# Weights of three projections moved by 4 to 28 bytes (a few by 128 or 256) against the operand that streams past them, and three raw buffers in place of four

## The chip, the cores and the metric

One core of one Trainium2 chip runs the whole program. The metric is the device time of one execution in microseconds, median of several runs.

## The reference

The reference is a decoder trunk of four layers over 256 tokens of width 1024. Each layer has a token mixer (Mamba-2 in layers 0 and 3, a gated linear recurrence in layer 1, a gated delta rule in layer 2), a cross-attention into 256 memory tokens, and a gated MLP. Cut to what matters here:

```python
for i in range(DEPTH):
    hn = rmsnorm(x, ln_mix[i])
    mix = (mamba2_mixer, hgrn2_mixer, gated_deltanet_mixer)[i % 3](hn, ...)   # begins with hn @ in_w, ends with @ out_w
    x = x + mix
    x = x + memory_cross_attention(rmsnorm(x, ln_xattn[i]), rmsnorm(mem, ln_mem[i]), ...)
    x = x + conv_glu_ffn(rmsnorm(x, ln_ffn[i]), f_up[i], f_conv_w[i], f_conv_b[i], f_down[i])

def conv_glu_ffn(h, up_w, conv_w, conv_b, down_w):
    gate, up = jnp.split(h @ up_w, 2, axis=-1)
    gate = causal_dwconv(gate, conv_w) + conv_b
    return (jax.nn.silu(gate) * up) @ down_w
```

All of it is float32. The weights of `in_w` (of the Mamba mixer), `up_w` and `down_w` are the ones the change touches; the kernel calls them `m_in`, `f_up` and `f_down`.

## The kernel before, in words

Every large product is done as three products of a shorter float format (float32r). A float32 operand is split into a high part H, which ScalarE writes as a cast, and a low part L, the rest, which VectorE writes as a difference; then `mm3` (lines 166 to 170) adds H·H, H·L and L·H into one PSUM bank. So one tile of weights of 128x1024 costs 24 matmuls: eight slices of 128 columns are loaded one after the other as the stationary operand, and 256 tokens stream past each of them three times.

`prep` (lines 152 to 164) brings such a tile in. It takes a buffer `raw` out of a ring of `WB[0]` = 4, one `wH` out of 3 and one `wL` out of 3, loads 512 KB over SyncE's queue (line 159), casts on ScalarE (line 160) and subtracts on VectorE (line 161). The framework adds the waits: a load waits until the difference that read its raw buffer is done, a cast waits until the matmuls that read its `wH` are done. `prep` runs at a higher priority than what stands around it, so the scheduler puts its load, cast and difference early on each engine's queue; each engine then works strictly in the order of its queue, SyncE's too.

The users of `prep` that matter here are these. `proj` (line 229) multiplies the layer's normalized input `hH`, `hL` with two tiles at a time; the Mamba mixer calls it for `m_in` (line 619, eight groups g of six tiles in each of layers 0 and 3, into the bank `mps`) and the MLP for `f_up` (line 475, 44 tiles per layer, bank `ffps`). `out_proj` (line 254) multiplies a mixer's or the MLP's result, split into `aH` and `aL`, with `f_down` (and other weights) in groups of four tiles, into the four banks `acc`; in the MLP it has six groups, the last of half size. The other products with weights (`xa_kv`, `xa_q`, `xa_o`, `h_in`, `g_in`, `g_out`, `m_out`, `h_out`) use the same `prep`.

Where the tiles lie in a partition of SBUF is settled when the program is built. Here the buffers `raw`, `wH` and `wL` begin at multiples of 512 bytes; `hH`, `hL`, `aH`, `aL` and the memory's `mH`, `mL` begin 192 bytes past such a multiple (the tile `apad` of 48 floats puts `aH` there). A slice of weights is 512 bytes long and a row of tokens 1024. So in nearly every product of `mm3` the address of the streamed operand less that of the loaded one is 192 modulo 512 bytes, and this number is what "distance" means in this document. It is 320 where the weights stream and the tokens are loaded (half of `xa_kv`, and one part of `h_in`), and 0 in the scores of the attention (bank `sc`).

The delta-rule mixer of layer 2 (lines 829 to 1126) needs a small triangular inverse per head: VectorE makes `MT`, SyncE's queue writes it to a DRAM scratch `gd` (line 927) and reads blocks of it back as `blk` (line 928), GpSimd works on them and writes them to DRAM, and SyncE's queue brings `U` back (line 958). These loads stand in the same queue as the raw loads. Around them a class `Weave` lets the heads' small matmuls slip between the projections' matmuls by a clock of its own.

Of the kernel before, what the change touches and what calls it, by code (L numbers as in the profile page):

```python
# [9 lines left out]
F32R = mybir.dt.float32r  # L10
# [6 lines left out]
P = 128  # L17
D = 1024
T = 256
# [3 lines left out]
NFF = 22  # L23
# [63 lines left out]
def tile_trunk(ctx: ExitStack, tc: tile.TileContext, io: dict, out: bass.AP, layers=range(DEPTH), parts="mxf", final=True):  # L87
    nc = tc.nc
    ACT, DVE, POOL, PE = nc.scalar, nc.vector, nc.gpsimd, nc.tensor
    weave = Weave()  # L90
    WB = [4,3,3]
    HL = [607, 282, 1973, 470, 14335, 1000]
    NL = [9214]
    LAT = [21000, 5620, 1450, 1042, 1588, 1117, 1724, 2353, 942, 2058, 8335, 1093, 4452, 2125, 1556]
# [6 lines left out]
    wp = ctx.enter_context(tc.tile_pool(name="wp", bufs=3))  # L101
# [12 lines left out]
    def bank(name):  # L114
        return ps_acc.tile([P, 512], F32, tag="acc", name=name)
# [8 lines left out]
    def f32(ap):  # L124
        return ap.bitcast(F32)
# [23 lines left out]

    between = []  # L150

    def prep(src, n=1024, step=1024):
        with tc.high_priority(offset=PRIO):
            raw = wp.tile([P, 1024], F32, tag="raw", name="raw", bufs=WB[0])
            H = wp.tile([P, 1024], F32R, tag="wH", name="wH", bufs=WB[1])
            L = wp.tile([P, 1024], F32R, tag="wL", name="wL", bufs=WB[2])
            for o in range(0, n, step):
                c = slice(o, min(n, o + step))
                nc.sync.dma_start(out=raw[:, c], in_=src[:, c])
                ACT.copy(H[:, c], raw[:, c])  # L160
                DVE.tensor_tensor(out=L[:, c], in0=raw[:, c], in1=f32(H[:, c]), op=ALU.subtract)  # L161
                if len(between) > 1:
                    between[-1](between.pop(0))
        return H, L

# [5 lines left out]

    def split(src, H, L):
        return (ACT.copy(H, src), DVE.tensor_tensor(out=L, in0=src, in1=f32(H), op=ALU.subtract))  # L173

# [5 lines left out]

    def split_gain(src, g, H, L):

# [43 lines left out]
        yield 440, 0  # L226


    def proj(srcs, ps):

        for i, s in enumerate(srcs):
            H, L = prep(s)
            for kt in range(KT):
                c = slice(kt * P, (kt + 1) * P)
                mm3(ps[:, i * T:(i + 1) * T], H[:, c], L[:, c], hH[:, kt, :], hL[:, kt, :],
                    i == 0 and kt == 0, kt == KT - 1)
                if kt % 2:
                    weave.tick(654)
# [12 lines left out]
                    if k % 2:  # L251
                        weave.tick(654)

    def out_proj(wsrc, nk, a, gens=None, gname=None, layer=0, last=False):


        accs = [bank(f"acc{b}") for b in range(4)]
        ng = (nk + 3) // 4
        st = Stats(DVE if last else POOL)
        for g in range(ng):  # L260
            n = min(4, nk - 4 * g)
            if gens is not None:
                weave.finish(gens[g])
            aH, aL = [], []
            for k in range(0, n, 2):
                H = ap_.tile([P, 2, T], F32R, tag="aH", name="aH")
                L = ap_.tile([P, 2, T], F32R, tag="aL", name="aL")
                split(a[:, 4 * g + k:4 * g + k + 2, :], H, L)
                aH += [H[:, 0, :], H[:, 1, :]]
                aL += [L[:, 0, :], L[:, 1, :]]  # L270
            for b in range(4):
                H, L = prep(wsrc[g, b], n * T)
                for cb in range(2):
                    for k in range(n):
                        kt = 4 * g + k
                        c = slice(k * T + cb * P, k * T + (cb + 1) * P)
                        mm3(accs[b][:, cb * T:(cb + 1) * T], H[:, c], L[:, c], aH[k], aL[k],
                            kt == 0 and cb == 0, kt == nk - 1)
                        if k % 2:
                            weave.tick(654)  # L280
                if g == ng - 1:
                    xs = flat(xT[:, 2 * b:2 * b + 2, :])
                    DVE.tensor_tensor(out=xs, in0=xs, in1=accs[b], op=ALU.add)
                    if gname is not None:
                        for kt in (2 * b, 2 * b + 1):
                            split_gain(xT[:, kt, :], pcol(gname, layer * 8 + kt), hH[:, kt, :], hL[:, kt, :])
                    st.add(xs)
                    if last:
                        for kt in (2 * b, 2 * b + 1):
                            fg = pcol("final", kt)  # L290
                            if b < 3:
                                POOL.tensor_scalar(out=KTt[:, kt, :], in0=xT[:, kt, :], scalar1=fg, scalar2=None, op0=ALU.mult)
                            else:
                                ACT.activation(out=KTt[:, kt, :], in_=xT[:, kt, :], func=AF.Copy, scale=fg)
        return st
# [161 lines left out]
    def ffn(layer, st, hook=None, last=False):  # L457
        with ExitStack() as ex:
            wk = ex.enter_context(phase(f"ff{layer}", 2))
            aT = wk.tile([P, NFF, T], F32, name="aT", bufs=1)  # L460
            rs = np_.tile([P, T], F32, tag="nrs", name="nrs", bufs=1)
            def gate(t, ps):
                gu = wk.tile([P, 2, T], F32, tag="gu", name="gu")
                DVE.tensor_tensor(out=gu, in0=ps.rearrange("p (a b) -> p a b", a=2),
                                  in1=rs.unsqueeze(1).to_broadcast([P, 2, T]), op=ALU.mult)
                c = wk.tile([P, T], F32, tag="c", name="c")
                conv(c, gu[:, 0, :], lambda j: pcol("f_cw", (layer * NFF + t) * 3 + j), 3, pcol("f_cb", layer * NFF + t))
                silu = ACT.activation(out=c, in_=c, func=AF.Silu)
                DVE.tensor_tensor(out=aT[:, t, :], in0=c, in1=gu[:, 1, :], op=ALU.mult)
                return silu  # L470

            todo = []
            for t in range(NFF):
                ps = bank("ffps")
                proj([io["f_up"][layer, 2 * t + i] for i in range(2)], ps)
                todo.append((t, ps))
                if t == 0:
                    continue
                if t == 1:
                    st.rs(rs)  # L480
                for u in todo:
                    silu = gate(*u)
                todo = []
                if t == 6 and hook is not None:
                    hook(silu)
            exp_ln_tables(silu)
            return out_proj(io["f_down"][layer], NFF, aT, last=last)

    def softplus(u, n, tmp):

# [18 lines left out]
    def mamba(layer, ia, gname):  # L509
        with ExitStack() as ex:  # L510
# [5 lines left out]
            H, L = prep(io["m_dt"][ia], 256)  # L516
# [94 lines left out]
            gens = []  # L611
            for g in range(8):
# [3 lines left out]
                Es = [wk.tile([P, 384], F32, tag=f"E{k}", name="E") for k in range(4)]  # L616
                for u in range(3):
                    ps = bank("mps")
                    proj([io["m_in"][ia, 6 * g + 2 * u + i] for i in range(2)], ps)
                    with tc.high_priority(offset=EVAC):  # L620
                        if u == 2:
                            exp_ln_tables(ACT.activation(out=bx, in_=cc, func=AF.Silu),
# [537 lines left out]
    for i, l in enumerate(layers):  # L1160
# [7 lines left out]
        else:  # L1168
            for kt in range(KT):
                g = "ln_xattn" if "x" in parts else "ln_ffn"  # L1170
# [13 lines left out]
    for b in range(4):  # L1184
        o = Vt.rearrange("p a (b t) -> p (a b) t", t=T)[:, 2 * b:2 * b + 2, :]
# [125 lines left out]
```

## Time and profile before

| | us |
|---|---|
| median of 3 runs | 2073.72 (2066.06 to 2088.24) |
| the profiled execution | 2072.47 |
| its span, first to last instruction | 2070.7 |
| TensorE busy | 2025.5 |
| VectorE busy | 1590.6 |
| ScalarE busy | 1282.5 |
| GpSimd busy | 344.5 |

The mean granted clock of TensorE was 0.997. TensorE's matmuls are recorded from the moment they begin to stream until their result is written, so one lasts longer (about 280 ns) than the step to the next; PE is the row of the matmuls, PEld that of the weight loads. A row of the timeline gives the start, the duration, the engine, the line and the names "written <- read".

### The profile page before, as it was taken

To read this page: it belongs to the slowest core of one execution; us is meant where nothing else is said; L and a number is where in the kernel's file an instruction comes from. 1 tells how busy PE (TensorE), PEld (TensorE's weight loads), DVE (VectorE), ACT (ScalarE), POOL (GpSimd) and SP (SyncE) were. 2 spreads that over 40 slices of the span, in tenths; PEclk is the share of its full clock that TensorE was granted. 3 is DMA by queue.
4 is the path that set the end of the run, shared out by engine and by line. 5 is a ranking of instruction groups with operands and counts; after the bars stand their busy time and mean duration, and the time that the engine had idled before them with its cause. 6 is when DMAs were issued, how large, how long until landed. Compare 5 with 4: busy or idle time off the path is not lost.

```text
span 2070.7 us, 42162 instructions
## 1 busy us (share of the span) xinstructions
PE 2025.5 (98%) x17084; PEld 1971.5 (95%) x17084; DVE 1590.6 (77%) x2423; ACT 1282.5 (62%) x1874; POOL 344.5 (17%) x468
## 2 busy tenths in 40 slices
PE   8999999999999999999999999999999999999997
PEld 8999999999999899999988889999999999999997
DVE  6899787875688777866786775778757999778765
ACT  6677666654565566555676875666545777666553
POOL 2032211000132110001064451110000223201001
PEclk9999999999999999999999999999999999999999
DMA  7554555655654446666543333456656444545663
GB/s 239 163 155 152 162 154 162 206 188 170 206 157 140 149 137 195 203 195 192 186 130 126 114 113 115 139 163 211 195 179 196 151 154 150 174 133 183 186 189 115
DMA packets 110372, 343.10 MB, mean 166 GB/s; under 512 B 15456, under 2 KB 25312, under 8 KB 110176
## 3 DMA queue, kind: packets, MB, share of 16 engines
q1 hardware_dynamic: 106176, 333.42, 52.0%
q10 hardware_dynamic: 3744, 6.71, 1.0%
q8 instruction: 134, 2.20, 0.4%
q0 software_dynamic: 256, 0.26, 0.1%
q14 instruction: 62, 0.51, 0.1%
HBM read 336.42 MB, written 3.93 MB: 164 GB/s over the span
## 4 chain that ended last, share of the span: by engine, by line
PE 79%; DVE 6%; issue 5%; ACT 4%; DMA 3%; POOL 2%; ACTq 0%; SPq 0%; DVEq 0%; POOLq 0%
PE acc L168 7%; PE ffps L170 7%; PE acc L169 7%; PE ffps L169 7%; PE ffps L168 7%; PE acc L170 7%; PE mps L168 4%; PE mps L169 4%; PE mps L170 4%; DVE wL L161 2%; PE kvps L170 2%; PE kvps L168 2%; PE kvps L169 2%; PE qps L170 2%; PE qps L168 2%
## 5 line engine op out<-in xcount | busy, mean ns | idle before, releaser
L161 DVE TENSOR_TENSOR wL<-raw,wH 128x1024 fp32r<-128x1024 f32 (+2 forms) x639 | 776.1, 1216 | 318.9 <-ACT wH L160 316.6
L160 ACT CAST wH<-raw 128x1024 fp32r<-128x1024 f32 (+2 forms) x639 | 658.4, 1031 | 510.6 <-PE ffps L169 156.4
L168 PE MATMUL acc<-aH,wH 128*128 128x256 f32 x1408 | 396.4, 282 | 0.6 <-ACT aH L173 0.6
L170 PE MATMUL ffps<-hH,wL 128*128 128x256 f32 x1408 | 392.6, 279 | 1.8 <-DVE wL L161 1.7
L168 PE MATMUL ffps<-hH,wH 128*128 128x256 f32 x1408 | 392.0, 279 | 2.5 <-ACT hH L183 2.5
L170 PE MATMUL acc<-aH,wL 128*128 128x256 f32 x1408 | 393.0, 279 | 0.0
L169 PE MATMUL acc<-aL,wH 128*128 128x256 f32 x1408 | 392.4, 279 | 0.1
L169 PE MATMUL ffps<-hL,wH 128*128 128x256 f32 x1408 | 392.1, 279 | 0.2
L168 PEld LDWEIGHTS ffps<-hH,wH 128*128 128x128 f32 x1408 | 265.5, 189 | 3.4 <-ACT hH L183 3.3
L168 PEld LDWEIGHTS acc<-aH,wH 128*128 128x128 f32 x1408 | 265.2, 189 | 3.5 <-issue 1.3
L170 PEld LDWEIGHTS ffps<-hH,wL 128*128 128x128 f32 x1408 | 264.4, 188 | 4.1 <-DVE wL L161 3.7
L169 PEld LDWEIGHTS acc<-aL,wH 128*128 128x128 f32 x1408 | 265.6, 189 | 1.5 <-issue 0.5
L169 PEld LDWEIGHTS ffps<-hL,wH 128*128 128x128 f32 x1408 | 265.1, 188 | 1.1 <-DVE hL L184 0.6
L170 PEld LDWEIGHTS acc<-aH,wL 128*128 128x128 f32 x1408 | 264.6, 188 | 0.4 <-DVE wL L161 0.2
L168 PE MATMUL mps<-hH,wH 128*128 128x256 f32 x768 | 219.8, 286 | 0.0
L170 PE MATMUL mps<-hH,wL 128*128 128x256 f32 x768 | 215.0, 280 | 0.0
L169 PE MATMUL mps<-hL,wH 128*128 128x256 f32 x768 | 214.9, 280 | 0.0
L203 POOL TENSOR_TENSOR ns<-nsq 128x256 f32<-128x256 f32 x13 | 10.5, 811 | 856.5 <-ACT nsq L200 856.5
L168 PEld LDWEIGHTS mps<-hH,wH 128*128 128x128 f32 x768 | 145.1, 189 | 2.7 <-issue 2.4
L170 PEld LDWEIGHTS mps<-hH,wL 128*128 128x128 f32 x768 | 145.4, 189 | 0.1
L169 PEld LDWEIGHTS mps<-hL,wH 128*128 128x128 f32 x768 | 144.5, 188 | 0.3
L170 PE MATMUL gps<-hH,wL 128*128 128x256 f32 x448 | 127.2, 284 | 0.9 <-DVE wL L161 0.9
(397 smaller groups left out, 4489.9 us busy)
## 6 DMA issues: line engine op xcount, KB each, us to landing
raw<-f_up SPq DMA_DIRECT2D x176, 512.0 KB, 3.6
raw<-m_in SPq DMA_DIRECT2D x96, 512.0 KB, 3.5
raw<-f_down SPq DMA_DIRECT2D x80, 512.0 KB, 3.5
raw<-xa_kv SPq DMA_DIRECT2D x60, 512.0 KB, 4.2
raw<-g_in SPq DMA_DIRECT2D x48, 512.0 KB, 3.9
raw<-m_out SPq DMA_DIRECT2D x32, 512.0 KB, 3.5
raw<-xa_q SPq DMA_DIRECT2D x32, 512.0 KB, 3.5
raw<-xa_o SPq DMA_DIRECT2D x32, 512.0 KB, 3.5
```

The source lines that it names most:

```text
L160: ACT.copy(H[:, c], raw[:, c])
L161: DVE.tensor_tensor(out=L[:, c], in0=raw[:, c], in1=f32(H[:, c]), op=ALU.subtract)
L168: PE.matmul(dst, aH, bH, start=start, stop=False, skip_group_check=True)
L169: PE.matmul(dst, aH, bL, start=False, stop=False, skip_group_check=True)
L170: PE.matmul(dst, aL, bH, start=False, stop=stop, skip_group_check=True)
L203: self.eng.tensor_tensor(out=self.sum, in0=sq[:, :T], in1=sq[:, T:], op=ALU.add)
```

## The change

Two things are changed. The ring of raw buffers has three tiles in place of four. And `wH` and `wL` become 512 bytes longer each, with the weights put o elements into them, where o is chosen by a new argument `far`: the distance is then `far` in place of 192. `m_in` gets one distance for each of the eight groups in each of its two layers (144 matmuls each), `f_up` one for each half of its 22 steps in each layer (528 each), and `f_down` one for each half of its groups in each layer (288 for the first, 240 for the second). Together these are 2304 + 4224 + 2112 = 8640 of the 15512 matmuls of the float32r kind. All other products keep 192, 320 or 0 (and the small `m_dt` and `g_ba`, whose slices are 128 and 192 bytes long, the distances that change from slice to slice): what lies behind the weights moves down by 1024 bytes, a multiple of 512.

```diff
-    WB = [4,3,3]
+    WB = [3,3,3]
...
+    FAR = 192
+    UP = [(176, 184), (188, 196), (200, 208), (216, 168)]
+    DOWN = [(196, 200), (208, 188), (184, 176), (448, 320)]
+    MIN = [(164, 168, 172, 176, 180, 184, 188, 448), (196, 200, 204, 208, 212, 216, 220, 64)]
+
+    def prep(src, n=1024, step=1024, far=FAR):
+        o = (FAR - far) % 512 // 4
         with tc.high_priority(offset=PRIO):
             raw = wp.tile([P, 1024], F32, tag="raw", name="raw", bufs=WB[0])
-            H = wp.tile([P, 1024], F32R, tag="wH", name="wH", bufs=WB[1])
-            L = wp.tile([P, 1024], F32R, tag="wL", name="wL", bufs=WB[2])
+            H = wp.tile([P, 1152], F32R, tag="wH", name="wH", bufs=WB[1])[:, o:o + 1024]
+            L = wp.tile([P, 1152], F32R, tag="wL", name="wL", bufs=WB[2])[:, o:o + 1024]
...
-    def proj(srcs, ps):
+    def proj(srcs, ps, far=FAR):
...
-            H, L = prep(s)
+            H, L = prep(s, far=far)
...
-    def out_proj(wsrc, nk, a, gens=None, gname=None, layer=0, last=False):
+    def out_proj(wsrc, nk, a, gens=None, gname=None, layer=0, last=False, fars=(FAR, FAR)):
...
-                H, L = prep(wsrc[g, b], n * T)
+                H, L = prep(wsrc[g, b], n * T, far=fars[2 * g // ng])
...
-                proj([io["f_up"][layer, 2 * t + i] for i in range(2)], ps)
+                proj([io["f_up"][layer, 2 * t + i] for i in range(2)], ps, UP[layer][2 * t // NFF])
...
-            return out_proj(io["f_down"][layer], NFF, aT, last=last)
+            return out_proj(io["f_down"][layer], NFF, aT, last=last, fars=DOWN[layer])
...
-                    proj([io["m_in"][ia, 6 * g + 2 * u + i] for i in range(2)], ps)
+                    proj([io["m_in"][ia, 6 * g + 2 * u + i] for i in range(2)], ps, MIN[ia][g])
```

The order of the instructions stays as it is over most of the program. TensorE's differs in one stretch alone, in the delta-rule mixer. SyncE's queue differs there too. At its beginning, around the load of the first inverse (`U` from the scratch `gd_12485`), SyncE has before:

```order
L159 DMA raw<-g_in 128x1024 x4
L958 DMA U<-gd_12485 128x4x128
L159 DMA raw<-g_in 128x1024
L927 DMA gd_12484<-MT 128x4x128
L928 DMA blk<-gd_12484 32x16x16
L159 DMA raw<-g_in 128x1024 x3
L958 DMA U<-gd_12486 128x4x128
```

and after (lines 8 higher):

```order
L167 DMA raw<-g_in 128x1024 x3
L966 DMA U<-gd_12485 128x4x128
L167 DMA raw<-g_in 128x1024
L935 DMA gd_12484<-MT 128x4x128
L167 DMA raw<-g_in 128x1024
L936 DMA blk<-gd_12484 32x16x16
L167 DMA raw<-g_in 128x1024 x3
L966 DMA U<-gd_12486 128x4x128
```

One raw load that stood ahead of `U` now stands two places behind it. At the mixer's end, where the loads of its output weights `g_out` begin, SyncE has before:

```order
L958 DMA U<-gd_12486 128x4x128
L159 DMA raw<-g_in 128x1024 x2
L159 DMA raw<-g_out 128x1024 x2
L927 DMA gd_12483<-MT 128x4x128
L159 DMA raw<-g_out 128x1024
L928 DMA blk<-gd_12483 32x16x16
```

and after:

```order
L966 DMA U<-gd_12486 128x4x128
L167 DMA raw<-g_in 128x1024 x3
L167 DMA raw<-g_out 128x1024
L935 DMA gd_12483<-MT 128x4x128
L167 DMA raw<-g_out 128x1024
L936 DMA blk<-gd_12483 32x16x16
```

The sequence is the same, shifted by one load.

## Rows read from the trace of the kernel before

**Rows 1.** Page: busy us (share of span) and instructions of each engine.

```profile
PE 2025.5 (98%) x17084; PEld 1971.5 (95%) x17084; DVE 1590.6 (77%) x2423; ACT 1282.5 (62%) x1874; POOL 344.5 (17%) x468
```

**Rows 2.** Groups of instructions on PE, 440 to 520 us.

```profile
L169 PE MATMUL acc<-aL,wH 128*128 128x256 f32 x174 | 48.9, 281 | 0.0
```

**Rows 3.** Groups of instructions on PE, 880 to 950 us.

```profile
L169 PE MATMUL acc<-aL,wH 128*128 128x256 f32 x168 | 46.4, 276 | 0.0
```

**Rows 4.** Timeline of ScalarE, layer 0's MLP, 460 to 472 us.

```profile
464.16 1.05 ACT L160 CAST wH<-raw 128x1024 fp32r<-128x1024 f32 x1 [0.16 <-PE acc L169]
466.98 1.05 ACT L160 CAST wH<-raw 128x1024 fp32r<-128x1024 f32 x1 [1.77 <-PE acc L169]
```

**Rows 5.** Timeline of ScalarE, layer 1's MLP, 905 to 925 us.

```profile
909.35 1.05 ACT L160 CAST wH<-raw 128x1024 fp32r<-128x1024 f32 x1 [1.67 <-PE acc L169]
912.07 1.05 ACT L160 CAST wH<-raw 128x1024 fp32r<-128x1024 f32 x1 [1.67 <-PE acc L169]
```

**Rows 6.** Busy time by stretch: us, PE busy (matmuls), granted clock, DMA share, GB/s.

```profile
346.00:386.00 40.00, 40.00 (x355) 1.00 0.65 205
...
440.00:520.00 80.00, 80.00 (x681) 1.00 0.57 178
...
880.00:950.00 70.00, 70.00 (x620) 1.00 0.62 182
...
1480.00:1540.00 60.00, 60.00 (x531) 1.00 0.59 181
1900.00:1980.00 80.00, 80.00 (x682) 1.00 0.61 188
1985.00:2055.00 70.00, 70.00 (x597) 1.00 0.50 160
```

**Rows 7.** Groups by form on PE, 60 to 76 us (Mamba mixer, layer 0).

```profile
L169 PE MATMUL mps<-hL,wH 128*128 128x256 f32 x45 | 12.4, 276 | 0.0
```

**Rows 8.** Groups by form on PE, 1640 to 1760 us (Mamba mixer, layer 3).

```profile
L169 PE MATMUL mps<-hL,wH 128*128 128x256 f32 x277 | 77.7, 280 | 0.0
```

**Rows 9.** Tile sc, PE: duration ns min/median/max, first and last start.

```profile
L169 PE MATMUL sc<-k1L,qH x16: 283/283/283, 293.0 to 1831.8; 128*128 128x256 f32 x16
```

**Rows 10.** Tile dtps, PE and PEld, loads of 32 columns.

```profile
L169 PEld LDWEIGHTS dtps<-hL,wH x16: 107/108/109, 56.6 to 1596.5; 128*32 128x32 f32 x16
L169 PE MATMUL dtps<-hL,wH x16: 276/276/280, 56.7 to 1596.6; 128*32 128x256 f32 x16
```

**Rows 11.** Tile acc, PEld, loads of 128 columns, 440 to 570 us.

```profile
L168 PEld LDWEIGHTS acc<-aH,wH x176: 187/188/188, 458.3 to 520.1; 128*128 128x128 f32 x176
```

**Rows 12.** Groups by form on VectorE: differences and convolution taps.

```profile
L304 DVE SCALAR_TENSOR_TENSOR cc<-mps,prm,cc 128x255 f32<-128x255 f32 x64 | 30.5, 476 | 0.1
...
L304 DVE SCALAR_TENSOR_TENSOR cc<-mps,prm,cc 128x253 f32<-128x253 f32 x64 | 30.3, 474 | 0.9
```

**Rows 13.** Timeline of VectorE, layer 1's MLP, 905 to 925 us.

```profile
910.43 1.23 DVE L161 TENSOR_TENSOR wL<-raw,wH 128x1024 fp32r<-128x1024 f32 x1 [1.49 <-ACT wH L160]
```

**Rows 14.** Page: DMA issues, count, KB each, median us to landing.

```profile
raw<-f_down SPq DMA_DIRECT2D x80, 512.0 KB, 3.5
```

**Rows 15.** Waits of SyncE's queue: us in total, times, longest us.

```profile
SPq L159 <- DVE wL L161: 1235.3, 470, 7.0
...
SPq L958 <- DMA gd<-ub: 88.6, 8, 16.1
```

**Rows 16.** Timeline of SyncE's queue in the delta-rule mixer.

```profile
1062.99 2.16 SPq L159 DMA_DIRECT2D raw<-g_in  x3
1081.31 0.38 SPq L958 DMA_DIRECT2D U<-gd  x1
```

**Rows 17.** Busy by stretch, delta-rule mixer: us, PE, PEld, DVE, ACT, POOL, clock, DMA, GB/s.

```profile
1070.00:1080.00 10.00, 9.98 (x88) 9.54 (x88) 6.27 (x11) 5.57 (x9) 8.15 (x20) 1.00 0.00 0
1080.00:1090.00 10.00, 8.14 (x65) 7.20 (x64) 4.89 (x10) 4.26 (x7) 3.64 (x6) 1.00 0.57 153
1090.00:1100.00 10.00, 7.64 (x52) 7.43 (x52) 5.50 (x9) 4.49 (x6) 8.26 (x23) 0.83 0.43 171
```

More of the change, by code (lines that the diff above doesn't have):

```diff
@@ L150, in tile_trunk @@
     between = []
-    def prep(src, n=1024, step=1024):
+    FAR = 192
[4 more added lines that the diff above has]
+        o = (FAR - far) % 512 // 4
         with tc.high_priority(offset=PRIO):
             raw = wp.tile([P, 1024], F32, tag="raw", name="raw", bufs=WB[0])
-            H = wp.tile([P, 1024], F32R, tag="wH", name="wH", bufs=WB[1])
-            L = wp.tile([P, 1024], F32R, tag="wL", name="wL", bufs=WB[2])
+            H = wp.tile([P, 1152], F32R, tag="wH", name="wH", bufs=WB[1])[:, o:o + 1024]
+            L = wp.tile([P, 1152], F32R, tag="wL", name="wL", bufs=WB[2])[:, o:o + 1024]
             for o in range(0, n, step):
```

## The prediction

> **What bounds the kernel now.** I read the page's first part first: matmuls cover 98% of the span and weight loads 95%, VectorE 77%, ScalarE 62% [rows 1]. Nobody is waited for long, so the time is the number of matmuls times the step from one to the next, plus small gaps.
>
> Then I looked at that step, by groups of instructions in stretches. The same instruction of the same shape lasts 281 ns in layer 0's MLP and 276 ns in layer 1's, with no idle time ahead of it in either [rows 2, 3] and a granted clock of 1.00 in both [rows 6], the level of 2.4 GHz. ScalarE's casts show what that means for the step: a cast starts when 24 matmuls have freed its buffer, and the casts are 2.82 us apart in the one and 2.72 us in the other [rows 4, 5]. So the step is 117.5 ns or 113.3 ns. I call these the slow and the fast level; they differ by 4.2 ns. The reader is to see that both occur at one and the same distance, 192, that a level lasts for hundreds of matmuls, and that it changes only at a disturbance: counts by stretch are at the fast level until 386 us (355 in 40 us), at the slow one from 440 to 520 (681 in 80), fast through layers 1 and 2 (620 in 70, 531 in 60), slow in layer 3 (682 in 80, 597 in 70) [rows 6]. In the Mamba mixers `m_in` is fast at the beginning (276 ns) and mostly slow later (280 ns, four of the five ns) [rows 7, 8]. So the distance alone does not settle the level here; some phase between weight load and stream does.
>
> Two more rows bear on it. At distance 0, the attention's scores, a matmul lasts 283 ns at the median of the group shown, a third level [rows 9]; by the same proportion (7 ns against 5 for a step of 4.2) its step is 5.9 ns above the fast one. And for `m_dt`, whose loads are of 32 columns (108 ns in place of 188 [rows 10, 11]) and whose distances are 192, 64, 448 and 320 in turn, it lasts 276 ns at the median [rows 10]. Four distances and a far shorter load give no step below the fast level. I take 113.3 ns as the floor of this shape.
>
> **The change part by part.** The sum is made on the profiled execution, 2072.5 us: 2070.7 of span and 1.8 around it. The median of the runs, 2073.7, is 0.1% above.
>
> *The distances.* They touch 8640 matmuls. How many of these are slow now: in layer 0 those from about 400 to 520 us, 120 / 0.1175 = 1020; in layer 3's MLP all 1584; of the 2304 for `m_in` all but the first 133, at four fifths, some 1740. Together 4340, half of the 8640. If every new distance gave the fast level, the gain would be 4340 x 4.2 ns = 18.2 us. If every one gave the slow level, the loss would be the other 4300 x 4.2 ns = 18.1 us. If every one gave the level of distance 0, the loss would be 8640 x 5.9 ns - 18.2 us = 33 us. No row shows a distance between 160 and 220 other than 192, so these are the ends. I take 0, the middle of the first two: 32 pieces of 144 to 528 matmuls at as many distances should fall on both levels, as 192 itself does, and the nearest rows are those of 192, half and half.
>
> *What weights off the old grid cost.* Distances such as 164 or 196 start the weights a few bytes past a 16-byte multiple. For ScalarE and VectorE, which write these tiles, I take nothing: taps of the convolution that write one and three floats off the tile's start take 476 and 474 ns [rows 12], and both engines have slack. For the weight load no row shows such a start. From above: 128 columns take 188 ns and 32 take 108 [rows 10, 11], 0.83 ns for each column, so a load that had to fetch four columns' worth more would take 3.3 ns more. Not counting distances divisible by 16, 5952 matmuls are touched (1728 of `m_in`, 3168 of `f_up`, 1056 of `f_down`): 19.6 us. From below: nothing, or a gain counted above already. I take 0, because a load 80 ns shorter did not shorten the step [rows 10]: at the fast level the load's length isn't what ends last.
>
> The Trainium skill, in "SBUF — State Buffer" under "Specifications (TRN2)", says that SBUF is read in lines of 16 bytes and that each cross to a new line pays a penalty. Weights that start inside a line would cross one line more per load; no row here shows whether that is felt, and by that rule the sum would lean to the upper end of 19.6 us.
>
> *Three raw buffers in a steady stretch.* The load of a tile is issued when the difference of the tile four before is done; SyncE's queue waits for VectorE 470 times, 1235 us in total [rows 15], and that wait is harmless now. With three it is issued one tile earlier in the ring: after the difference that ends at 910.43 + 1.23 = 911.66 us [rows 13], for the cast three steps after 909.35, at 909.35 + 3 x 2.72 = 917.51 [rows 5]. That leaves 5.85 us, of which landing takes 3.5 [rows 14]: 2.3 us to spare, against 5.1 now. So the cover holds, by half its size. Where other loads share the queues (the program's start, the memory's loads in each MLP) it can fail for a tile or two: 0 to 4 us, and I take 1, since three `wH` buffers still stand between a late cast and TensorE.
>
> *Three raw buffers in the delta-rule mixer.* Here SyncE's queue stands still for `U`, 88.6 us in 8 waits, the longest 16.1 [rows 15], and no raw load behind it is issued. The reader can see one such wait: three raw loads are issued by 1065.2, and `U` follows at 1081.3 [rows 16]. TensorE lives on its stock (9.98 of 10 us busy with no DMA at all), then falls to 8.14 and 7.64, and the granted clock to 0.83 [rows 17]. The stock is now one tile smaller, 24 steps, 2.7 us. It costs that for each wait that outlasts the stock. Ends: at most half of the eight, 11 us, since their mean of 11.1 lies well under the longest; and below, a gain of 2.7 us where the shifted order lets a head's chain start a tile earlier. I take one such stall and one drop of the clock like that of the row (10 us x 0.17 = 1.7 us): 4.4 us.
>
> Sum: 2072.5 + 0 + 0 + 1 + 4.4 = 2077.9, rounded 2078 us. The first term's ends alone, all fast and all slow, put it at 2060 and 2096; all ends together at 2052 (2072.5 - 18.2 - 2.7) and 2140 (2072.5 + 33 + 19.6 + 4 + 11).
>
> **The rivals.** *All fast.* Each new distance takes away the slow level. For it: a level is stable for a thousand matmuls, so it is a property of how load and stream meet, and an address shifts that. Against it: distances 192 and 320 have not done it, and `m_in` falls to the slow level again and again. It gives 2077.9 - 18.2 = 2060 us, and 2054 without the raw ring's 5.4; even that is within 1% of before, because of the floor.
>
> *Locked slow.* Load and stream meet badly at most of the new distances, at the slow level or at that of distance 0. For it: 283 ns at distance 0 shows that a distance can hold a level [rows 9]. Against it: 192, 64, 448 and 320 all reach 276 ns. It gives 2077.9 + 18.1 = 2096 us if all are slow, and 2111 if all are like distance 0; it decides the sign from 16.6 us (2094.5 less 2077.9), when the mean step of the 8640 is (18.2 + 16.6) / 8640 = 4.0 ns above the fast level: nearly all slow, or fewer slow with some at the third level.
>
> *Longer loads.* The 3.3 ns of the off-grid start are paid in full: 2077.9 + 19.6 = 2098 us. Against it stands the 32-column load that gained nothing.
>
> *The distance does nothing.* The levels come from the stalls alone, every stretch keeps the level that it has, and only the ring counts: 2078 us, 2073 to 2084.
>
> The Trainium skill, in "TensorE: Matmul & The Clock Gate" under "Step-by-step: what each phase is for", says that TensorE has two independent read ports and that loading the next weights takes nothing from the matmul that runs. By that rule the last rival holds and no distance could matter. The trace speaks against it in part: 283 ns at distance 0 beside 276.
>
> **How the numbers follow.** Mixed levels, my forecast: 0.45, with its own range 2064 to 2094. All fast 0.12. Locked slow 0.20, longer loads 0.10, distance without effect 0.13. About 1% is what a measurement of this kernel can tell from no change, 20.7 us: below 2053 or above 2094.5. Faster by that much needs all fast and a gain in the delta-rule mixer: 0.05. Slower needs locked slow (three quarters of it), longer loads (most of it) or a bad end of the mixed case: 0.27. The same: 0.68. The range reaches from all fast to two thirds of the way into locked slow: 2058 to 2106 us.
>
> **What would show it.** The matmuls' mean duration by group and stretch: 276, 281 or 283 ns for `ffps` by layer and half, for `mps` by group and for `acc`. Right, if both 276 and 281 appear among the new distances and no group of a thousand matmuls lies above 283. Wrong, if a duration below 276 appears with a step below 113.3 ns (then the floor is none), or if off-grid groups lie at 284 and aligned ones (176, 208, 448) at 281 or less (longer loads). For the ring: casts in layer 1's MLP still released by TensorE, not by a DMA, and in the delta-rule mixer PE's busy time in its 290 us lower by 2 to 6 us. The prediction fails as a whole if the time is under 2058 or over 2106.

## The result, and the profile after

| | before | after |
|---|---|---|
| median, us | 2074.89 (2063.97 to 2088.24, 16 runs) | 2092.49 (2089.39 to 2098.16, 16 runs) |
| the profiled execution | 2072.47 | 2090.15 |
| its span | 2070.7 | 2088.3 |

The ratio of after to before is 1.0094, with a 95% interval of 1.0074 to 1.0113: the change makes the kernel 0.9% slower (the two medians alone give 1.0085). The spread is as telling as the median: the changed kernel's runs lie within 9 us, those of before within 24.

The page of after, first part, beside [rows 1]:

```profile
PE 2042.6 (98%) x17084; PEld 1990.5 (95%) x17084; DVE 1590.6 (76%) x2423; ACT 1282.8 (61%) x1875; POOL 342.0 (16%) x468
```

The counts and the shares on TensorE are as before, and PE is busy 17.1 us longer (2042.6 less 2025.5), nearly all of the 17.6 us that the span grew. TensorE's idle time is as long as before in sum (45.7 us of the span against 45.2), though, as shown below, not in the same places. So the same matmuls take longer.

Which of them, the windows of after show, beside [rows 6]. The columns are us, PE busy (matmuls), PEld, DVE, ACT, POOL, granted clock, DMA share, GB/s. From the top: `f_up` at 184, 196, 200, 208, 216 and 168, then `f_down` at 448 and 320:

```profile
405.00:455.00 50.00, 50.00 (x425) 50.00 (x425) 39.06 (x55) 25.73 (x36) 0.00 (x0) 1.00 0.64 198
...
845.00:895.00 50.00, 50.00 (x421) 50.00 (x420) 38.42 (x54) 25.49 (x36) 0.00 (x0) 1.00 0.65 190
1391.00:1441.00 50.00, 50.00 (x425) 49.95 (x424) 40.86 (x61) 31.91 (x48) 0.00 (x0) 1.00 0.62 200
1452.00:1502.00 50.00, 50.00 (x427) 50.00 (x426) 38.72 (x54) 25.86 (x36) 0.00 (x0) 1.00 0.63 191
1903.00:1953.00 50.00, 50.00 (x420) 49.95 (x420) 41.09 (x59) 30.56 (x44) 0.00 (x0) 1.00 0.58 183
1962.00:2012.00 50.00, 50.00 (x444) 50.00 (x443) 40.07 (x57) 26.68 (x37) 0.00 (x0) 1.00 0.63 193
...
2020.00:2048.00 28.00, 28.00 (x249) 28.00 (x248) 15.48 (x16) 15.12 (x17) 0.00 (x0) 1.00 0.65 190
2052.00:2074.00 22.00, 22.00 (x197) 22.00 (x196) 10.58 (x13) 8.59 (x11) 0.28 (x1) 1.00 0.38 121
```

TensorE is busy all through each of them and the clock is granted in full. A window also counts the two or three matmuls that reach over its edges (0.28 us each, 2.4 steps), so 50 / (444 - 2.4) = 113.2 ns a step at 168, 117.8 to 118.3 at 208, 200 and 184 (427, 425), and more at 196 (421, 119.4 ns) and 216 (420). Such a count can be off by one or two at the edges; ScalarE's casts, 24 matmuls apart, don't depend on that. In after, beside [rows 4, 5], with `f_down` at 188 first and `f_up` at 168 below:

```profile
945.49 1.05 ACT L168 CAST wH<-raw 128x1024 fp32r<-128x1024 f32 x1
948.33 1.05 ACT L168 CAST wH<-raw 128x1024 fp32r<-128x1024 f32 x1 [1.79 <-PE acc L177]
...
1962.66 1.05 ACT L168 CAST wH<-raw 128x1024 fp32r<-128x1024 f32 x1 [1.35 <-PE ffps L177]
1965.38 1.05 ACT L168 CAST wH<-raw 128x1024 fp32r<-128x1024 f32 x1 [1.17 <-PE ffps L177]
```

2.84 / 24 = 118.3 ns and 2.72 / 24 = 113.3. The casts are still released by TensorE, in layer 1 and layer 3 alike, and not by a DMA.

`m_in` in after, groups by form at 60 to 76 us and at 1640 to 1760, beside [rows 7, 8]:

```profile
L177 PE MATMUL mps<-hL,wH 128*128 128x256 f32 x45 | 12.7, 281 | 0.0
...
L177 PE MATMUL mps<-hL,wH 128*128 128x256 f32 x273 | 76.6, 281 | 0.0
```

What was 276 ns at the beginning is 281 now, and the 280 of layer 3 are 281.

The rest of the time is in the delta-rule mixer. A window over the whole of it, from its first projection matmul to its last, in after:

```profile
1006.00:1240.00 234.00, 218.19 (x1763) 205.44 (x1762) 181.67 (x360) 175.65 (x262) 95.97 (x221) 0.99 0.42 130
```

and in before:

```profile
1003.00:1233.00 230.00, 218.31 (x1761) 205.17 (x1760) 184.92 (x364) 175.16 (x262) 101.81 (x228) 0.99 0.41 127
```

The work is the same, 218 us, and the idle time goes from 11.7 to 15.8 us. Where it is, the waits of TensorE in after say (waiter, releaser: us in total, times, longest):

```profile
PE l L891 <- ACT gsq L888: 7.6, 1, 7.6
```

And one window of after there, beside [rows 17]:

```profile
1070.00:1080.00 10.00, 3.94 (x12) 2.91 (x13) 2.97 (x7) 6.25 (x9) 3.63 (x14) 0.68 0.65 219
```

And what `gsq` waited for, after's timeline of SyncE's queue and of ScalarE (beside [rows 16]):

```profile
1049.39 4.93 SPq L167 DMA_DIRECT2D raw<-g_in  x3
1066.86 0.38 SPq L966 DMA_DIRECT2D U<-gd  x1
1067.32 0.46 SPq L167 DMA_DIRECT2D raw<-g_in  x1
...
1072.49 1.04 ACT L168 CAST wH<-raw 128x1024 fp32r<-128x1024 f32 x1 [7.67 <-DMA raw<-g_in]
...
1074.09 1.28 ACT L197 ACT_TABLE_LOAD   x1
1075.38 0.63 ACT L888 ACTIVATE gsq<-qk 128x512 f32<-128x512 f32 x1
```

From 1054.3 to 1066.9 the queue stands still for `U`; the next raw loads come behind it, ScalarE has no tile to cast for 7.67 us, its `gsq` stands in its queue behind that cast, and TensorE uses up its stock, and falls to 3.94 us of 10, with a mean granted clock of 0.68 in the same window. In before the same wait for `gsq` is under 0.5 us. In this mixer ScalarE's and VectorE's orders differ from before too, and not only TensorE's and SyncE's; a load of a function table (ACT_TABLE_LOAD above, 1.28 us) stands between `qk` and `gsq` here, where before has none. So what is measured here is the ring of three together with the order that the scheduler made for it.

By stages, from the first matmul of each bank to the first of the next, the profiled executions differ like this: `f_up` +7.4 us in the four layers, `f_down` +3.4, `m_in` +1.3, together +12.1; the delta-rule mixer +3.9; all else +1.6. Together that is the 17.6 us of the span.

### The profile page after: what moved, and what is told of

Read it like the earlier page. It is cut to its first block, busy times and chain, and to the rows that moved or that the text cites. A ratio compares the mean times of both kernels' runs of the same rounds, so it can differ in the third digit from the quotient of the medians.

```text
span 2088.3 us, 42161 instructions
## 1 busy us (share of the span) xinstructions
PE 2042.6 (98%) x17084; PEld 1990.5 (95%) x17084; DVE 1590.6 (76%) x2423; ACT 1282.8 (61%) x1875; POOL 342.0 (16%) x468
## 4 chain that ended last, share of the span: by engine, by line
PE 82%; DVE 6%; issue 5%; ACT 3%; POOL 2%; DMA 2%; SPq 0%; DVEq 0%; ACTq 0%; POOLq 0%
PE ffps L177 8%; PE ffps L178 8%; PE ffps L176 8%; PE acc L176 7%; PE acc L177 7%; PE acc L178 7%; PE mps L176 4%; PE mps L178 3%; PE mps L177 3%; DVE wL L169 2%; PE kvps L176 2%; PE kvps L178 2%; PE kvps L177 2%; PE qps L178 2%; PE qps L177 2%
```

## The experiments

Two questions were open: what a distance does to the step (a property of the distance, of the off-grid start, of the order, or chance), and what the ring costs alone. Unless said otherwise the base is the changed kernel. "Step" is the mean interval between successive matmul starts, intervals over 130 ns left out (only at 196 does that hide something, see the table). Each ratio is to runs of the kernel before on the same chip. That kernel's median was between 2066.6 and 2075.6 us from chip to chip, so where two runs from two chips are a few microseconds apart, both the ratio and the time have to be looked at.

**One distance throughout, as before.**

```diff
-    UP = [(176, 184), (188, 196), (200, 208), (216, 168)]
-    DOWN = [(196, 200), (208, 188), (184, 176), (448, 320)]
-    MIN = [(164, 168, 172, 176, 180, 184, 188, 448), (196, 200, 204, 208, 212, 216, 220, 64)]
+    UP = [(192, 192)] * 4
+    DOWN = [(192, 192)] * 4
+    MIN = [(192,) * 8] * 2
```

> The changed kernel with every distance put back to 192; three raw buffers and the longer tiles stay. Theory (the distances made the loss): f_up, f_down and m_in show 276 and 281 ns side by side again, the time is that of the kernel before within 0.3% (2069 to 2081 us). Rival (the ring of three made it): the time stays at 2089 to 2098 us, and the loss shows as idle time of TensorE or as waits for DMA, not as a longer matmul.

Measured: 2075.63 us (2063.32 to 2084.45), ratio to before 1.0041 [1.0014, 1.0069]. The time is in the forecast range, but 0.4% is more than the 0.3% expected. The ring of three and the longer tiles are still in; the loss is less than half of the change's, and the wide spread is back. `f_up` of layer 0, first and second half, and of layer 3, second half:

```profile
344.00:394.00 50.00, 50.00 (x425) 49.95 (x425) 40.78 (x61) 31.30 (x48) 0.00 (x0) 1.00 0.64 198
...
402.00:452.00 50.00, 50.00 (x444) 50.00 (x443) 41.03 (x58) 27.48 (x39) 0.00 (x0) 1.00 0.69 206
...
1948.00:1998.00 50.00, 50.00 (x427) 50.00 (x426) 38.61 (x54) 25.57 (x36) 0.00 (x0) 1.00 0.62 189
```

Both levels at one distance, and layer 0 fast where before was slow there. TensorE's timeline shows where layer 0 changes its level:

```profile
397.24 0.28 PE L176 MATMUL ffps<-hH,wH 128*128 128x256 f32 x1
397.36 0.28 PE L177 MATMUL ffps<-hL,wH 128*128 128x256 f32 x1
397.51 0.39 PE L178 MATMUL ffps<-hH,wL 128*128 128x256 f32 x1
397.74 0.28 PE L176 MATMUL ffps<-hH,wH 128*128 128x256 f32 x1
```

Two starts come late, 0.15 and 0.23 us behind the one before; ahead of them the mean step is 117.8 ns, behind them 113.4. As to the change's loss: more than half of it lies in the distances (0.94% with them, 0.41% without).

**168 throughout**, the one that was fast in the change (the same three lines, with 168):

```diff
+    UP = [(168, 168)] * 4
+    DOWN = [(168, 168)] * 4
+    MIN = [(168,) * 8] * 2
```

> The changed kernel with 168 for every matmul of f_up, f_down and m_in, the one distance off 192 at which f_up ran at 276 ns throughout. Theory (each distance has its own level): f_up and f_down at 276 ns in all four layers, m_in near its 116.4 ns step; 8640 matmuls go from a mean of 117.2 ns to about 113.8 ns, so 2060 to 2066 us, below the kernel before. Rival (168 was only lucky in the phase it met): one to three of the four layers at 281 ns or more, 2070 to 2095 us.

Measured: 2070.27 us (2061.99 to 2088.57), ratio 1.0014 [0.9986, 1.0041]. `f_up` of layers 1 and 2, second half:

```profile
846.00:896.00 50.00, 50.00 (x419) 50.00 (x418) 37.65 (x54) 25.12 (x35) 0.00 (x0) 1.00 0.61 186
...
1448.00:1498.00 50.00, 50.00 (x444) 50.00 (x443) 41.37 (x59) 27.76 (x38) 0.00 (x0) 1.00 0.69 207
```

A miss: 168 isn't fast by itself. It has two levels, 113.3 and 120.0 ns (419), and this execution took the slow one in layers 0, 1 and 3.

**216 throughout**, which stepped 119.2 ns in the change (the same lines, with 216):

```diff
+    UP = [(216, 216)] * 4
+    DOWN = [(216, 216)] * 4
+    MIN = [(216,) * 8] * 2
```

> The changed kernel with 216 for all three weights, whose steps were 119.2 ns in f_up and in m_in. Theory (each distance has its own level): 119.2 ns in all 8640, 282 ns a matmul, 8640 x (119.2 - 117.2) = 17 us above the changed kernel: 2105 to 2113 us. Rival (levels come from the stalls): a mixture of 276 and 281 ns, 2075 to 2095 us.

Measured: 2102.61 us (2101.54 to 2104.55), ratio 1.0185 [1.0160, 1.0211]. Each of the four layers shows this row or one within two matmuls of it:

```profile
1969.00:2019.00 50.00, 50.00 (x422) 50.00 (x421) 38.36 (x53) 25.08 (x35) 0.00 (x0) 1.00 0.60 188
```

119.0 to 119.2 ns in every product changed, and four runs that agree within 3 us. The levels came as forecast; the time stayed 2.4 us under the forecast range (2105 to 2113). So a distance can hold a slow level, and where there is one level the spread goes.

**The two halves exchanged**, to part the distance from the place:

```diff
-    UP = [(176, 184), (188, 196), (200, 208), (216, 168)]
-    DOWN = [(196, 200), (208, 188), (184, 176), (448, 320)]
+    UP = [(184, 176), (196, 188), (208, 200), (168, 216)]
+    DOWN = [(200, 196), (188, 208), (176, 184), (320, 448)]
```

> The changed kernel with the two halves of f_up and of f_down exchanged in each layer. Theory (each distance has its own level): the steps move with their distances, layer by layer: 168 at 113.3 ns, now first in layer 3, 216 at 119.2 ns behind it, 176 at 118.7, 184 at 118.3, 208 at 117.8; the time stays within 3 us of the changed kernel, except for f_down of layer 3 (448 and 320): if these two only keep the level that they meet, they stand behind 216 now and lose 528 x 4.4 ns = 2.3 us. Rival (the place in the program sets the level): the second half of layer 3 is again at 113.3 ns and the others stay as they were.

Measured: 2088.54 us, one run. In layer 3 `f_up` at 168 comes first now and 216 behind it, then `f_down` at 320:

```profile
1900.00:1950.00 50.00, 50.00 (x441) 49.95 (x440) 43.03 (x62) 32.15 (x46) 0.00 (x0) 1.00 0.63 192
1959.00:2009.00 50.00, 50.00 (x422) 50.00 (x421) 38.02 (x54) 25.21 (x35) 0.00 (x0) 1.00 0.60 182
...
2020.00:2045.00 25.00, 25.00 (x214) 25.00 (x214) 13.62 (x13) 11.57 (x13) 0.00 (x0) 1.00 0.60 189
```

The levels went with the distances: 168 fast in either place, 216 slow in either, and so for the other six of `f_up` within 0.6 ns. One did not: 320, fast behind 448 in the change, is slow behind 216 (25 / (214 - 2.4) = 118.1 ns), while 448 behind it is fast again (113 to 114 ns from its first step on, with no late start ahead of it). So 320 has two levels as well. That the time stayed within 3 us of the changed kernel, as forecast, one run can't tell.

**448 throughout** (the same lines, with 448):

```diff
+    UP = [(448, 448)] * 4
+    DOWN = [(448, 448)] * 4
+    MIN = [(448,) * 8] * 2
```

> The changed kernel with 448 for every matmul of f_up, f_down and m_in. Theory (a distance has a set of levels, and 448 has the fast one alone for long runs, since f_down at 448 was fast behind a slow 320 too): f_up and f_down at 276 ns in all four layers, m_in near 115.9 ns a step, about 12 us under the kernel with all at 192: 2060 to 2067 us. Rival (448 keeps what it meets, like 192): one to three layers at 281 ns, 2066 to 2085 us.

Measured: 2077.46 us (2068.91 to 2085.81), ratio 1.0019 [0.9997, 1.0041]. `f_up` of layers 0 and 1, second half:

```profile
404.00:454.00 50.00, 50.00 (x427) 50.00 (x427) 39.13 (x55) 25.83 (x36) 0.00 (x0) 1.00 0.64 198
...
838.00:888.00 50.00, 50.00 (x444) 50.00 (x443) 41.17 (x58) 27.39 (x39) 0.00 (x0) 1.00 0.67 207
```

Another miss: 448 is fast or slow by chance, as 192 is.

**204 throughout** (the same lines, with 204), a distance that was mostly fast in `m_in` (step 115.0 among neighbours at 117.7 to 119.8):

```diff
+    UP = [(204, 204)] * 4
+    DOWN = [(204, 204)] * 4
+    MIN = [(204,) * 8] * 2
```

> The changed kernel with 204 for all three weights: m_in's group at 204 ran at 115.0 ns, the least of all its groups off 192. Theory (a set of levels for each distance): m_in at 115.0 ns in both layers; f_up and f_down at one level throughout or at two, one of them 113.3 ns; 2058 to 2080 us. Rival (204 is like its neighbours 200 and 208): 117.8 ns in f_up and f_down, 2085 to 2095 us.

Measured: 2061.71 us (2056.62 to 2073.51), ratio 0.9959 [0.9939, 0.9980]: faster than both kernels. `f_up` of layer 0, second half, and the other three layers lie within a matmul of it:

```profile
399.00:449.00 50.00, 50.00 (x444) 50.00 (x443) 41.08 (x59) 27.53 (x39) 0.00 (x0) 1.00 0.68 206
```

**The ring alone**, on the kernel before:

```diff
-    WB = [4,3,3]
+    WB = [3,3,3]
```

> The kernel before with three raw buffers in place of four, nothing else. Theory (the ring costs some microseconds, nearly all of them in the delta-rule mixer): that stage, from its first matmul to its output weights, lasts 232 to 240 us in place of 230, the granted clock falls to half there for 6.8 us or more in place of 3.4, all other stages differ by their levels alone; the time is 3 to 9 us above the kernel before. Rival (the 0.4% of the kernel with all at 192 is luck of the levels): no difference beyond 0.15%, 3 us.

Measured: 2076.58 us (2070.12 to 2090.78), ratio 1.0012 [0.9990, 1.0034]. The forecast of 3 to 9 us is missed: by the time the ring can't be told from nothing, as the rival said, since the levels' chance is wider than it. The waits of TensorE show it:

```profile
PE l L883 <- ACT gsq L880: 6.7, 1, 6.7
```

That wait is 6.7 us here with the distances of before. The mixer takes 232.0 us, the lower end of the forecast, against 230.1 in before, and the granted clock is at its half level (1.2 GHz) for 6.8 us in it, against 3.4 in before.

**The kernel before once more** (no edit), for what one kernel does from one execution to the next.

> The kernel before once more, for a second profile. Theory (at 192 the level of a stretch is settled by the stall ahead of it, anew in each execution): other layers of f_up and f_down at 281 ns than the first profile had (there layers 0 and 3), the stretches of m_in as they were; the delta-rule stage again within 2 us of 230. Rival (the program's order fixes the level): layers 0 and 3 at 281 and 1 and 2 at 276 ns again.

Measured: 2077.53 us. The same wait of TensorE:

```profile
PE l L883 <- ACT gsq L880: 0.7, 2, 0.4
```

And `f_up` of layers 1 and 2, second half:

```profile
838.00:888.00 50.00, 50.00 (x444) 50.00 (x443) 41.20 (x59) 27.28 (x39) 0.00 (x0) 1.00 0.67 206
...
1436.00:1486.00 50.00, 50.00 (x427) 50.00 (x426) 38.95 (x55) 25.57 (x36) 0.00 (x0) 1.00 0.63 193
```

Layer 2 is slow here; in the first profile of the same program it was fast (113.4 ns by the starts). So at 192 the level of a layer is drawn anew in each execution. The mixer took 229.9 us, and the long wait for `gsq` isn't there. Over the twelve profiles with a ring of three the wait for `gsq` is 6.6 to 7.9 us and the mixer took 231.7 to 240.7 us, 234.1 in the mean; with four it is 0.7 in both, and 230.1 and 229.9.

**204 for every product whose weights are loaded**, the mixers' and the attention's too:

```diff
-    def prep(src, n=1024, step=1024, far=FAR):
+    def prep(src, n=1024, step=1024, far=204):
```

(on top of 204 throughout; with `proj` and `out_proj` likewise, and 192 kept where the weights stream)

> The kernel with 204 for the three weights, and now 204 also for every other product whose weights are loaded (xa_q, xa_o, g_in, h_in's loaded parts, the mixers' output weights, half of xa_kv); weights that stream keep 192. Theory (204 has the fast level and keeps to it): the slow shares that are left in those products shrink, worth up to 5 us in all: 2055 to 2062 us, and 0.5 to 0.9% under the kernel before. Rival (in stretches with many stalls 204 does no better than 192): 2060 to 2064 us as with the three weights alone.

Measured: 2062.95 us (2056.22 to 2072.76), ratio 0.9994 [0.9972, 1.0015]. `f_up` of layers 0 and 1, second half:

```profile
398.00:448.00 50.00, 50.00 (x444) 50.00 (x443) 41.23 (x58) 28.06 (x39) 0.00 (x0) 1.00 0.70 207
...
832.00:882.00 50.00, 50.00 (x427) 50.00 (x426) 39.19 (x55) 26.01 (x36) 0.00 (x0) 1.00 0.67 194
```

So 204 has a slow level too (117.8), met in one of the eight MLP layers profiled at it so far. The forecast (2055 to 2062 us, and 0.5 to 0.9% under the kernel before) is missed: nothing more is gained in the other products.

**180 throughout** (the same lines, with 180):

```diff
+    UP = [(180, 180)] * 4
+    DOWN = [(180, 180)] * 4
+    MIN = [(180,) * 8] * 2
```

> The changed kernel with 180 for the three weights. In the changed kernel m_in's group at 180 had 61% of its steps at the fast level and a third above 119 ns. Theory (168, 180, 192 and 204, 12 bytes apart, have the fast level and a second one; the neighbours have no fast one): f_up and f_down show stretches of 113.3 ns and stretches of one slower level, 2060 to 2085 us. Rival (180 is like its neighbours 176 and 184): 118.3 to 118.7 ns throughout, 2092 to 2102 us.

Measured: 2060.21 us (2057.60 to 2064.61, ten runs), ratio 0.9979 [0.9959, 1.0000]. All four MLPs at 113.3 to 113.5 ns, without the slow stretches that the theory expected there, and a spread of 7 us. By the ratio 180 can't be told from the kernel before. `m_in` at 1640 to 1760 us, then one group of it at 143 to 148 and at 149.8 to 154.4:

```profile
L177 PE MATMUL mps<-hL,wH 128*128 128x256 f32 x272 | 75.7, 278 | 0.0
...
L177 PE MATMUL mps<-hL,wH 128*128 128x256 f32 x15 | 4.1, 276 | 0.0
...
L177 PE MATMUL mps<-hL,wH 128*128 128x256 f32 x13 | 3.7, 283 | 0.0
```

So 180 has a slow level too. In this group the first 47 steps are at 113.3 ns, then come eight matmuls of another kind (`cb`, `xt`), and some 40 steps behind them are at 120.0. Twelve of the sixteen groups show this, at the same place.

**180 in the MLP, 204 in `m_in`:**

```diff
+    UP = [(180, 180)] * 4
+    DOWN = [(180, 180)] * 4
+    MIN = [(204,) * 8] * 2
```

> f_up and f_down at 180, m_in at 204, all else as in the changed kernel. Theory (each distance has its own levels; 180 and 204 reach the fast one and seldom leave it): the MLP products at 276 ns in all four layers, m_in at 277 to 278, and 2055 to 2062 us, a few us under the two kernels with one distance throughout (2060.2 and 2061.7), with a spread of under 12 us. Rival (a level is drawn after each stall and 180 was lucky in its ten runs): one or two of the MLPs at 281 to 283 ns, 2064 to 2072 us, spread over 15 us.

Measured: 2060.98 us (2057.01 to 2068.44), ratio 0.9925 [0.9897, 0.9953]. `f_up` of layer 2, second half:

```profile
1440.00:1490.00 50.00, 50.00 (x444) 50.00 (x443) 41.45 (x59) 27.49 (x38) 0.00 (x0) 1.00 0.68 207
```

All four MLPs fast again, `m_in` at 114.8 and 114.5 ns. By the time it isn't faster than 180 or 204 throughout (its profiled execution, 2068.44 us, spent 240.7 us in the delta-rule mixer). By the ratio it is, but the kernel before had 2075.57 us beside it, and 2066.59 beside 180; which of the two to believe stays open.

**The changed distances in the MLP, 180 in `m_in`:**

```diff
-    MIN = [(164, 168, 172, 176, 180, 184, 188, 448), (196, 200, 204, 208, 212, 216, 220, 64)]
+    MIN = [(180,) * 8] * 2
```

> The change with m_in alone put back to a distance with a fast level (180); f_up and f_down keep the changed distances. Theory (the loss lies in the products themselves, by their distance): the MLPs keep their 281 to 283 ns except at 168, 320 and 448, m_in goes to 277 to 278 ns as at 180 before, and the time is that of the changed kernel less 2304 x some 2.7 ns = 6 us: 2084 to 2090 us, narrow spread. Rival (the many different distances disturb each other, a change from one to the next is what costs): without the sixteen distances of m_in the MLPs' levels move too, 2068 to 2080 us.

Measured: 2091.43 us (2086.25 to 2096.33), ratio 1.0077 [1.0048, 1.0105]. `f_up` at 208 and at 168:

```profile
1451.00:1501.00 50.00, 50.00 (x424) 50.00 (x424) 38.89 (x54) 25.84 (x36) 0.00 (x0) 1.00 0.61 194
...
1958.00:2008.00 50.00, 50.00 (x444) 50.00 (x443) 40.07 (x57) 26.45 (x37) 0.00 (x0) 1.00 0.62 195
```

The MLP keeps its levels without `m_in`'s sixteen distances beside it, so the rival falls. The two stages of `m_in` take 167.3 us each in place of 169.2 and 169.5, 4 us in all, but the median is only 1 us under the change's: a miss by 1.4 us (by the ratios it is 3.5 us under). And 208, which stepped 117.8 in the change, steps 118.3 here: it has two levels, both slow.

**All distances together.** Mean steps in ns, in stretches of over 100 matmuls without the stage's beginning, over all these profiles:

| distance | step |
|---|---|
| 164, 184, 188 | 118.3 to 118.4 |
| 196 | 119.4 to 119.6, of which one step in twelve or thirteen takes 130 to 135 ns (118.4 without these) |
| 172, 220 | 119.8 to 119.9 |
| 176 | 118.6 to 118.8 |
| 200, 212 | 117.7 to 117.8 |
| 208 | 117.8 to 118.3 |
| 216 | 119.0 to 119.2 |
| 168 | 113.3 or 120.0 |
| 192, 320, 448 | 113.3 or 117.8 |
| 204 | 113.3 or, seldom, 117.8 |
| 180 | 113.3 in the MLP; 113.3 and 120.0 in turn in `m_in`, mean 113.4 to 115.8 |

In `m_in` the groups at distances with two levels lie between them (168 at 116.4, 204 at 115.0, 448 at 115.9 in the change). 164, 172, 212 and 220 were seen in one group of `m_in` each, and 64 too (117.8); whether they have a fast level as well stays open. For 176, 184, 188, 196, 200 and 208 there are six stretches of `f_up` and `f_down` each, all slow; a fast level that comes seldom isn't excluded for them, but the 16 runs of the changed kernel lie within 9 us. Only 216 was run throughout.

## Why the prediction was right and where it was wrong

**Range and direction.** 2092.49 us lies in the range (2058 to 2106), and a change of 0.9% is under the 1% bound that the prediction took. But the forecast, 2078, is 14.4 us short, and the likeliest case was not the one that came: the range holds the result because it was drawn two thirds of the way into a rival, not because the forecast's mechanism held.

**The step that failed: the distances, taken as 0.** The prediction put the new distances half on each level, "as 192 itself does". By the matmuls' starts (each to the next, intervals over 150 ns left out), the time above the floor of 113.3 ns in the changed products was 4.8 us in `f_down`, 7.6 in `f_up` and 7.6 in `m_in` before, 20.1 together (the prediction had 18.2), and is 8.1, 19.1 and 10.3 after, 37.5 together. So the term was +17.4, close to its "all slow" end of 18.1. Of the 8640 matmuls only the 1056 at 168, 448 and 320 in layer 3 ran at the fast level, and parts of `m_in` at 168, 180, 448 and 204. The mistake was to see 192's two levels as what any distance does: most of its neighbours showed no fast level in any stretch. The rows allowed for it, since 283 ns in the scores was a case of a held level [rows 9], and the prediction gave it 0.20.

**What was given back.** Those 17.4 us became 12.1 in the stages' lengths, and most of the difference is in `f_up` (11.4 in its steps, 7.4 in its length). With the mixer's 3.9 and 1.6 elsewhere that gives 2072.5 + 12.1 + 3.9 + 1.6 = 2090.1, the profiled time. A window in layer 2's `f_up`, in before:

```profile
1374.00:1484.00 110.00, 109.21 (x957) 108.66 (x956) 90.46 (x132) 66.53 (x95) 0.00 (x0) 1.00 0.64 199
```

and in after:

```profile
1388.00:1498.00 110.00, 110.00 (x935) 109.95 (x934) 88.76 (x128) 64.96 (x93) 0.00 (x0) 1.00 0.62 196
```

At the fast level TensorE idles 0.79 us here; at the slow one it doesn't. In this stage the steps cost 4.6 us (1055 steps at 117.8 ns in place of 113.4) and the stage grew by 2.7.

**The floor** held: no stretch of over 100 matmuls of this shape, in any of the fourteen profiles, steps under 113.3 ns.

**Longer loads** fell. The weights at 176 and 208 start on a 16-byte multiple and step 118.7 and 117.8 to 118.3, no better than 188 or 196; 180 and 204 start off it and reach 113.3. By the Trainium skill's rule that each cross of a 16-byte line pays a penalty ("SBUF — State Buffer", "Specifications (TRN2)"), the off-grid ones, which cross one line more, could have taken longer; no run here shows such a penalty in the step.

**The distance does nothing** fell too: 216 throughout gives 2102.61 us and 180 throughout 2060.21, a difference of 42 us by addresses alone (by the ratios, 1.0185 and 0.9979, 2.1%). The Trainium skill ("TensorE: Matmul & The Clock Gate", "Step-by-step: what each phase is for") says that loading the next weights takes no read bandwidth of SBUF from the running matmul. As a rule for the time, by which no address could matter, the runs at 216 speak against it, with a step of 119.1 ns against 113.3; that read bandwidth is what is lost there, no run shows.

**Locked slow** came nearest, at 2096 for 2092.5. Its point of decision, a mean of 4.0 ns above the fast level, was passed (37.5 us / 8528 steps = 4.4 ns); it stayed under the 1% because of the 5.3 us given back (17.4 less 12.1).

**The ring.** In the steady stretch 1 us was taken; the casts are still released by TensorE in layers 1 and 3, so the cover held and the cost there is not seen. In the delta-rule mixer 4.4 us was taken, and 3.9 measured in this pair of profiles, 4.1 over all (234.1 less 230.0), with 1.6 to 10.6 in the single profiles. That this comes so near 4.4 is in part luck. The mechanism is as told, one stall behind `U` and a drop of the clock behind it, but for the change of order on ScalarE and VectorE, which the prediction left out. The idle time in it rose by 4.1 us, within the 2 to 6 foreseen. The sizes of the parts were off: the stall is 7.6 us and not 2.7, and part of it is made good in the mixer, where other waits of TensorE are shorter in turn (for `S` 1.5 us in place of 3.6, for `on` 1.3 in place of 2.8).

**The signs to look for.** "Both 276 and 281 appear" was fulfilled by layer 3 alone; as a test it was too weak to tell mixed levels from locked slow. The share at each level would have been the number to ask for.

## What to carry to other kernels

When TensorE is the bound, compare the step of one and the same matmul shape between stretches: two values without any wait mean that something other than the program's order sets it, here the address of the weights in SBUF, in steps of 4 bytes. Try a few addresses throughout, with several runs each, and take one with the fast level and a narrow spread. Here that is 180 (2060 us, ten runs within 7) or 204: 1.1% and 1.3% under the change by the ratios, but only 0.2% and 0.4% under the kernel before, and for 180 the interval reaches up to no gain at all. Don't judge a distance by one profile: 168, 192, 204, 320 and 448 show the fast level in one execution or layer and a slow one in the next.

## What the runs showed of the hardware that was not expected

- Each distance seen has its own small set of mean steps, from 113.3 to 120.0 ns, at the full granted clock. 168, 180, 192, 204, 320 and 448 have the fast one. The first four are 12 bytes apart, but 216, the next in that row, didn't show it in any product of its run. Why, and what decides between two levels, stays open; that it is a phase between load and stream, as the prediction says, no run shows.
- Where a distance has two levels, the level changes behind a break: in the forty MLP layers profiled at 192, 168, 448, 204 or 180 throughout, no stretch of 48 or more steps between late starts (140 ns and over) changes its level, and the longest have 1486 steps. The next execution of the same program may take the other level. At 192, 168 and 448, of twelve layers that were slow behind their beginning eleven met no further break that changed it and stayed slow. Of eleven fast ones in layers 0 to 2, which met late starts 360 to 430 steps further on, four were slow from there on. This fits the wide spread between runs: 24 us before, 7 at 180 and 3 in the four runs at 216.
- 320 was fast behind 448 and slow behind 216, as if the level were inherited from the product ahead; but 448 was fast behind the slow 320, so that isn't the rule. It is one case each and was not tried further.
- All these runs move the weights and leave the streamed operand where it is, so the distance and the weights' own address change together, and which of them counts isn't separated. One sign for the distance: in `xa_kv`, where the weights stream past the loaded memory, 320 comes about with other addresses than in `f_down`, and shows the same two levels. In before, layers 1 and 2 (117.9 and 113.1 ns):

```profile
544.00:566.00 22.00, 22.00 (x189) 22.00 (x188) 10.70 (x11) 10.39 (x14) 0.00 (x0) 1.00 0.65 191
975.00:997.00 22.00, 22.00 (x197) 22.00 (x196) 10.78 (x12) 10.13 (x15) 0.12 (x1) 1.00 0.62 191
```

- No run has four raw buffers together with the longer tiles, so whether the mixer's stall goes away at 180 with them stays open.
